# One encoder layer on one core: weight loads moved from SyncE to GpSimd, the splits of the first weights placed behind the first norm, the second half's statistics behind the first features

## Chip, core and metric

The kernel runs on one core of one Trainium2 chip. The metric is the device time of one execution in microseconds. The engines of the core are TensorE (PE in the profile; its weight loads are PEld), VectorE (DVE), ScalarE (ACT), GpSimd (POOL) and SyncE (SP), each with its own instruction queue that is worked off in order. DMA transfers are issued from such a queue (SPq, POOLq) and run on 16 DMA engines.

## What is computed

One layer of a post-norm encoder on 1024 tokens of width 1024, all in float32. Cut to what matters here:

```python
x = layer_norm(x, ln_in_g, ln_in_b)
proj = x @ w_in[l]                       # (1024, 2304): q, k, v of three head groups
qa, ka, va, qb, kb, vb, qc, kc, vc = jnp.split(proj, split_points, axis=-1)
oa = neighbourhood_attention(qa, ka, va, na_rpb[l])        # group A, 4 heads
ob = sliding_window_gqa(qb, kb, vb, sw_sink[l], sw_table)  # group B, 8 query heads, 2 key heads
oc = differential_attention(qc, kc, vc, ...)               # group C, 4 heads
mix = jnp.concatenate([oa, ob, oc], axis=-1) @ w_out[l]
x = layer_norm(alpha * x + mix, ln_mix_g[l], ln_mix_b[l])
hdn = jax.nn.relu(x @ w_ff1[l])
x = layer_norm(alpha * x + (hdn * hdn) @ w_ff2[l], ln_ff_g[l], ln_ff_b[l])
```

## The kernel before

**Precision.** Every float32 operand of a matmul is split in two: a high part (a cast to the format that TensorE takes, `fp32r`) and a low part (the operand less its high part). A product is three matmuls, high x high, high x low and low x high (`mm3`, L144). So every weight block is loaded, cast (`hi`) and subtracted (`lo`) before TensorE can use it.

**The head.** The eight blocks of 128 tokens x0 to x7 are loaded by SP (`load_x`). `ln_half` (L223) takes four of them: statistics on VectorE (L208, L215, L217), a power of -1/2 on GpSimd (L218), the normalisation on ScalarE (L234) or, for two of the first four, on VectorE (L228); then for each of eight column blocks (`dc`) four transposes on TensorE (L239), gain and offset on ScalarE (L241), the high part on VectorE (L246) or ScalarE (L244) and the low part on VectorE (L247). The result `xT[half]` is the feature-major input of all projections. `first_w` (L333) loads the first weights of the queries and keys of group C (QC, KC) and splits them, the cast on VectorE (L338), the subtraction on GpSimd (L339). `split_vc` (L379) splits the value weights of group C: cast on ScalarE (L383), subtraction on VectorE (in the helper `sub`, L130). `t5_vectors` makes position biases, `ln_rows_out` makes the residual rows on GpSimd (L257, L260) and stores them from there (L261).

**The projections.** `feat_pieces` (L344) projects 128 columns of `w_in` in two pieces, one for each half of the tokens; its matmuls are `mm_feat`. `proj_tok` projects values. The first pieces are written out by hand: QC and KC of the first half, then the values of t = 0 to 3, the second half's features, QC and KC of the second half, the values of t = 4 to 7. All other projections (the second blocks of QC and KC, then QA, KA, VA, KB, VB, QB) stand in a list `bg` from which `run_bg` takes pieces at a low priority, as filler work, while the attention runs. Their weights come through `split_w` (L150): SP loads into a tile `raw` that has one buffer, ScalarE casts (L159), GpSimd subtracts (L161; VectorE for the second blocks of QC and KC). `whi` and `wlo` have two buffers each. A load into `raw` can go out only when the subtraction of the weights before has read it; until then SP's queue waits, with all that is behind it. Four blocks of `w_out` (6 and 7 as filler, 4 and 5 in the B stage) go the same way.

**The stages behind.** 32 steps of group C (`c_scores`: scores L471, a fused add and minimum on VectorE L474, exponential on ScalarE L478, the weighted sum of two softmaxes on GpSimd L485, L486 and VectorE L487; three steps later `c_trans` with transposes L500; later `c_values` L515), 16 steps of group A (L618 to L657), 16 of group B (L725 to L763), the output projection, the second norm, and two feed-forward products in seven instead of eight block products (L967 and L1097).

**Order.** The order of the instructions on each queue is made when the kernel is built, by a planner that takes the written order as priority and goes by a model of durations. `tc.issue_after(ins)` adds that instructions traced in its block come behind `ins`, for those on the same engine as `ins` only.

Of the kernel before, what the change touches and what calls it, by code (L numbers as in the profile page):

```python
# [17 lines left out]
P = 128  # L18
# [59 lines left out]
def encoder_kernel(ctx: ExitStack, tc: tile.TileContext, A: dict, out: bass.AP):  # L78
# [71 lines left out]
    def split_w(src_ap, shape, dest=None, raw=None, pool=False):  # L150
        if raw is None:
            raw = sb.tile(shape, F32, tag="raw", bufs=1, name=nm("raw"))
        load(out=raw, in_=src_ap)
        if dest is None:
            hi = sb.tile(shape, F32R, tag="whi", bufs=2, name=nm("whi"))
            lo = sb.tile(shape, F32R, tag="wlo", bufs=2, name=nm("wlo"))
        else:
            hi, lo = dest
        nc.scalar.copy(out=hi, in_=raw)  # L159
        eng = nc.gpsimd if pool else nc.vector  # L160
        eng.tensor_tensor(out=lo, in0=raw, in1=f32(hi), op=ALU.subtract)  # L161
        return hi, lo
# [60 lines left out]
    def ln_half(xs, half, cols):  # L223

        for j in range(4):
            mean, rstd = ln_stats(xs[j])
            if half == 0 and j % 2:
                nc.vector.tensor_scalar(out=xs[j], in0=xs[j], scalar1=mean, scalar2=rstd,  # L228
                                        op0=ALU.subtract, op1=ALU.mult)
# [3 lines left out]
            with (tc.issue_after(last_sub[0].ins) if half else ExitStack()):  # L233
                nc.scalar.activation(out=xs[j], in_=xs[j], func=AF.Identity, scale=rstd, bias=nmr)  # L234
        res = []
        for dc in range(8):
# [11 lines left out]
            if dc < 5:  # L248
                last_sub[0] = lo
            res.append(xp)  # L250
        return res

    def ln_rows_out(xs, rows, ydram):

        with tc.issue_after(last_pow[0].ins):
# [72 lines left out]
    def mm_feat(w, half):  # L328
        pm = ps_mm()
        mm3(pm, [(w[0][:, k, :], w[1][:, k, :], xT[half][k][:, 0, :], xT[half][k][:, 1, :]) for k in range(8)])  # L330
        return pm

    def first_w(base):  # L333
        raw = page([P, 8, P])
        load(out=raw, in_=w_cols(w_in, base, P))
        hi = sb.tile([P, 8, P], F32R, tag="whi", bufs=2, name=nm("whi"))
        lo = sb.tile([P, 8, P], F32R, tag="wlo", bufs=2, name=nm("wlo"))
        nc.vector.tensor_copy(out=hi, in_=raw)  # L338
        nc.gpsimd.tensor_tensor(out=lo, in0=raw, in1=f32(hi), op=ALU.subtract)  # L339
        return hi, lo  # L340

    def feat_pieces(base, f, scale, banded=False, w=None, pool=True):

        w = list(w or ())  # L344
# [57 lines left out]
    def va_pieces():  # L402
        w = []

        def piece(t):
            if not w:
                w.extend(split_v(VA))
# [1049 lines left out]
```

## Time and profile before

| | us |
|---|---|
| median of 3 runs | 1192.36 (1191.1 to 1193.9) |
| profiled execution, whole time | 1192.13 |
| its span, first to last instruction | 1190.4 |
| PE busy in the span | 1141.3 (96%) |
| DVE busy | 953.1 (80%) |
| ACT busy | 642.1 (54%) |
| POOL busy | 414.6 (35%) |
| PE in the chain that ended last | 79% |

Times in the rows are counted from the start of the span. "Busy" is time in which an instruction of the engine ran; matmuls overlap by part of their duration, so the pitch from one start to the next is shorter than the duration of one. A row of the time order has the start, the time until the last of its merged instructions ended, the engine, the line, the operation, output and input tiles with their shapes, the count, and in brackets how long the engine had been idle and what released it.

### The profile page before, as it was taken

How to read it: one execution, taken by the hardware profiler on the slowest of the kernel's cores; microseconds unless marked ns; L12 is line 12 of the kernel's file. 1: busy time of each engine (PE TensorE's matmuls, PEld its weight loads, DVE VectorE, ACT ScalarE, POOL GpSimd, SP SyncE). 2: the span in 40 equal slices, each digit the busy share in tenths (PEclk: the TensorE clock that was granted, in tenths of full speed). 3: DMA queues.
4: the chain of work that ended last, by engine and by line, in shares of the span. 5: the costliest groups of instructions: out<-in, count | busy, mean ns of one | idle time of the engine just before them, and what ended most of it. 6: DMA issues, size and time to landing. Idle time of an engine off the chain costs nothing.

```text
span 1190.4 us, 17144 instructions
## 1 busy us (share of the span) xinstructions
PE 1141.3 (96%) x5642; PEld 947.8 (80%) x5642; DVE 953.1 (80%) x1858; ACT 642.1 (54%) x1253; POOL 414.6 (35%) x368
## 2 busy tenths in 40 slices
PE   3999999999998989998999999999999999999996
PEld 2788889878877878876788888888888888888885
DVE  7566899998656688976779998999774988787985
ACT  4435666666556887765664544445553444444530
POOL 3875666685665775430121222222210000000201
PEclk9999999999989989999999999999999999999998
DMA  8566845362878971214376687766599754355731
GB/s 278 154 237 207 263 143 172 113 171 89 264 212 239 223 168 54 89 71 125 117 237 211 226 277 264 258 246 233 185 333 348 225 197 163 115 164 181 232 122 71
DMA packets 139408, 228.46 MB, mean 192 GB/s; under 512 B 11884, under 2 KB 76300, under 8 KB 139320
## 3 DMA queue, kind: packets, MB, share of 16 engines
q1 hardware_dynamic: 123800, 178.60, 47.7%
q0 software_dynamic: 15520, 48.77, 11.9%
q8 instruction: 45, 0.74, 0.3%
q14 instruction: 43, 0.35, 0.1%
HBM read 157.54 MB, written 77.60 MB: 198 GB/s over the span
## 4 chain that ended last, share of the span: by engine, by line
PE 79%; DVE 5%; ACT 3%; issue 2%; POOL 0%; DMA 0%; SPq 0%; DVEq 0%; ACTq 0%; POOLq 0%
PE psm L144 15%; PE psS L967 11%; PE psS L1097 11%; PE pst L967 7%; PE psm L967 7%; PE pst L1097 5%; PE psm L1097 5%; PE pspv L1097 4%; PE pspv L515 2%; PE psS L471 2%; PE pst L500 2%; PE pspv L754 1%; DVE pg L130 1%; PE pspv L652 1%; PE psS L725 1%
## 5 line engine op out<-in xcount | busy, mean ns | idle before, releaser
L144 PE MATMUL psm<-pg,whi 128*128 128x512 f32 x448 | 153.5, 408 | 2.1 <-DVE pg L246 1.8
L218 POOL TENSOR_TENSOR bnve<-bnve,pw 128x1 f32<-128x1 f32 x24 | 22.5, 940 | 360.7 <-DVE bnve L217 357.5
L1097 PE MATMUL psS<-pg,pg 128*128 128x512 f32 x576 | 140.5, 389 | 0.0
L967 PE MATMUL psS<-pg,pg 128*128 128x512 f32 x576 | 136.2, 393 | 2.4 <-ACT pg L827 2.4
L967 PEld LDWEIGHTS psS<-pg,pg 128*128 128x128 f32 x576 | 108.6, 189 | 25.2 <-ACT pg L827 2.9
L1097 PEld LDWEIGHTS psS<-pg,pg 128*128 128x128 f32 x576 | 108.1, 188 | 22.4
L827 ACT CAST pg<-hr 128x512 fp32r<-128x512 f32 x112 | 69.3, 619 | 95.3 <-PE pst L1097 40.8
L144 PEld LDWEIGHTS psm<-pg,whi 128*128 128x128 f32 x448 | 84.2, 192 | 22.0 <-DVE pg L246 2.2
L478 ACT ACTIVATE pg<-pg,cst 128x1024 f32<-128x1024 f32 x64 | 73.9, 1154 | 51.4 <-DVE cst L474 48.4
L144 PE MATMUL psm<-pg,wlo 128*128 128x512 f32 x224 | 89.7, 401 | 0.8 <-POOL wlo L161 0.8
L967 PE MATMUL psm<-pg,pg 128*128 128x512 f32 x384 | 89.8, 389 | 0.0
L967 PE MATMUL pst<-pg,pg 128*128 128x512 f32 x384 | 89.6, 389 | 0.0
L828 DVE TENSOR_TENSOR pg<-hr,pg 128x512 fp32r<-128x512 f32 x112 | 76.7, 685 | 13.0 <-ACT pg L827 12.9
L967 PEld LDWEIGHTS psm<-pg,pg 128*128 128x128 f32 x384 | 72.1, 188 | 15.0
L967 PEld LDWEIGHTS pst<-pg,pg 128*128 128x128 f32 x384 | 72.1, 188 | 15.0
L130 DVE TENSOR_TENSOR pg<-pst,pg 128x512 fp32r<-128x512 f32 (+2 forms) x112 | 64.9, 589 | 22.6 <-ACT pg L640 8.4
L485 POOL TENSOR_TENSOR pg<-pg,cst 128x704 f32<-128x704 f32 x32 | 49.2, 1537 | 80.1 <-DVE cst L482 52.7
L1097 PE MATMUL pst<-pg,pg 128*128 128x512 f32 x288 | 74.2, 389 | 0.0
L1097 PE MATMUL psm<-pg,pg 128*128 128x512 f32 x288 | 74.2, 389 | 0.0
L975 POOL DMA_DIRECT2D hd<-evb x80 | 43.2, 541 | 86.4 <-DVE evb L823 82.0
L144 PE MATMUL psm<-whi,pg 128*128 128x256 f32 (+1 forms) x256 | 71.5, 346 | 0.8 <-DVE pg L130 0.5
L827 ACT CAST pg<-evb 128x512 fp32r<-128x512 f32 x80 | 48.6, 617 | 39.5 <-DVE evb L823 39.4
(208 smaller groups left out, 2758.8 us busy)
## 6 DMA issues: line engine op xcount, KB each, us to landing
hr<-hd SPq DMA_DIRECT2D x28, 1024.0 KB, 5.7
hd<-evb POOLq DMA_DIRECT2D x80, 256.0 KB, 3.8
w1r<-in_w_ff SPq DMA_DIRECT2D x16, 1024.0 KB
evb<-in_w_ff SPq DMA_DIRECT2D x64, 256.0 KB, 3.7
qk<-evb SPq DMA_DIRECT2D x52, 256.0 KB, 3.9
y<-pg POOLq DMA_DIRECT2D x24, 512.0 KB, 4.4
pg<-y SPq DMA_DIRECT2D x24, 512.0 KB, 5.5
pg<-in_w_ff SPq DMA_DIRECT2D x32, 256.0 KB, 7.8
```

What stands on the lines that cost most here:

```text
L130: nc.vector.tensor_tensor(out=o, in0=a, in1=b, op=ALU.subtract)
L144: mm = nc.tensor.matmul(o, a, b, start=(i == 0), stop=(i == n - 1))
L471: last_mm[0] = nc.tensor.matmul(sc, q[:, m, (i % 2) * P:(i % 2) * P + P], kst[h][kh][:, m, :], start=True, stop=True)
L478: nc.scalar.activation(out=rt, in_=rt, func=AF.Exp, scale=-1.0, bias=sm[:, m:m + 1], accum_out=sm[:, 2 + m:3 + m])
L485: nc.gpsimd.tensor_tensor(out=R[1][:, a], in0=R[1][:, a], in1=sm[:, 6:7].broadcast_to([P, C_POOL]), op=ALU.mult)
L500: nc.tensor.transpose(pt[:, kb * P:(kb + 1) * P], src[:, c0:c0 + P], ident)
L515: nc.tensor.matmul(pv[:, 0:256], Vc[h // 2][kb // 4][:, kb % 4, h % 2, :], src[:, kb % 4, :], start=(n == 0), stop=(n == 15))
L827: nc.scalar.copy(out=pg[:, 0], in_=x)
L828: last_split[0] = nc.vector.tensor_tensor(out=pg[:, 1], in0=x, in1=f32(pg[:, 0]), op=ALU.subtract)
L967: nc.tensor.matmul(o, w[:, e, k], xo[m][k][:, f], start=(n == 0), stop=(n == 11))
L975: nc.gpsimd.dma_start(out=hd_d[m - 1, j], in_=x)
L1097: nc.tensor.matmul(o, h[:, e, sl], w[:, f], start=(k == 0 and n == 0), stop=(k == 15 and n == 2))
```

## The change

Three things. First, `split_w` is replaced by a class `Weights`: a chain in the order of use, in which the load of the next weights is issued right behind the split of those before, from GpSimd's queue where GpSimd did that subtraction, else from SP's. The blocks 6, 7, 4 and 5 of `w_out` are in the chain (`wout_chain`); blocks 0 to 3, which have pages of their own, are loaded by SP as before. Second, `first_w` is taken apart: `first_load` early, `first_split` after `ln_norm` of the first half, with the casts held behind the last normalisation on VectorE (`last_norm`) and the subtractions behind the last power on GpSimd (`last_pow`); the value weights of group C are loaded ahead of x4 to x7 and subtracted on GpSimd, and the first pieces use the low part of their weights last (`lo_last`). Third, `ln_half` is taken apart into `ln_norm` and `ln_feats`, and the second half's statistics are held behind the first half's features up to `dc` = 6 on VectorE.

```diff
-    def split_w(src_ap, shape, dest=None, raw=None, pool=False):
...
+    class Weights:
...
+        def load(self, eng):
+            self.raw = sb.tile(self.shape, F32, tag="raw", bufs=1, name=nm("raw"))
+            eng.dma_start(out=self.raw, in_=self.src)
+
+        def split(self):
+            if self.raw is None:
+                self.load(nc.sync)
+            hi = sb.tile(self.shape, F32R, tag="whi", bufs=2, name=nm("whi"))
+            lo = sb.tile(self.shape, F32R, tag="wlo", bufs=2, name=nm("wlo"))
+            nc.scalar.copy(out=hi, in_=self.raw)
+            eng = nc.gpsimd if self.pool else nc.vector
+            eng.tensor_tensor(out=lo, in0=self.raw, in1=f32(hi), op=ALU.subtract)
+            if self.next:
+                self.next.load(nc.gpsimd if self.pool else nc.sync)
+            return hi, lo
...
-    def ln_half(xs, half, cols):
+    def ln_norm(xs, half):
 
         for j in range(4):
-            mean, rstd = ln_stats(xs[j])
+            with (tc.issue_after(last_sub[0].ins) if half else ExitStack()):
+                mean, rstd = ln_stats(xs[j])
...
-            if dc < 5:
+            if dc < 7:
                 last_sub[0] = lo
...
-        with tc.issue_after(last_pow[0].ins):
+        with tc.issue_after(last_pool[0].ins), tc.issue_after(last_pow[0].ins):
...
+        if lo_last:
+            seq = [(0, e, k) for k in range(8) for e in (0, 1)] + [(1, 0, k) for k in range(8)]
...
+    def first_split(raws):
+
+        ws = []
+        for raw in raws:
+            hi = sb.tile([P, 8, P], F32R, tag="whi", bufs=2, name=nm("whi"))
+            with tc.issue_after(last_norm[0].ins):
+                nc.vector.tensor_copy(out=hi, in_=raw)
+            ws.append((hi, sb.tile([P, 8, P], F32R, tag="wlo", bufs=2, name=nm("wlo"))))
+        for raw, (hi, lo) in zip(raws, ws):
+            with tc.issue_after(last_pow[0].ins):
+                last_pool[0] = nc.gpsimd.tensor_tensor(out=lo, in0=raw, in1=f32(hi), op=ALU.subtract)
+        return ws
...
             nc.scalar.copy(out=hi, in_=raw)
-            sub(lo, raw, f32(hi))
+            with tc.issue_after(last_pool[0].ins):
+                last_pool[0] = nc.gpsimd.tensor_tensor(out=lo, in0=raw, in1=f32(hi), op=ALU.subtract)
...
-    qc = feat_pieces(QC, 0, CSC, w=first_w(QC))
-    kc = feat_pieces(KC, 0, 1.0, w=first_w(KC))
+    first_raws = [first_load(QC), first_load(KC)]
+    raws_vc = load_vc()
     load_x(range(4, NT))
-    raws_vc = load_vc()
     rows_in = ln_rows("ln_in")
-    xT[0] = ln_half(xs[0:4], 0, cols_in)
+    ln_norm(xs[0:4], 0)
+    first_ws = first_split(first_raws)
+    qc = feat_pieces(QC, 0, CSC, w=first_ws[0])
+    kc = feat_pieces(KC, 0, 1.0, w=first_ws[1])
+    xT[0] = ln_feats(xs[0:4], 0, cols_in)
     qc[0]()
     kc[0]()
+    wv = split_vc(raws_vc)
     t5_vectors()
-    wv = split_vc(raws_vc)
...
-    xT[1] = ln_half(xs[4:8], 1, cols_in)
+    ln_norm(xs[4:8], 1)
+    xT[1] = ln_feats(xs[4:8], 1, cols_in)
```

## Rows read from the trace of the kernel before

**Rows 1.** The page: engines' shares in the chain that ended last.

```profile
PE 79%; DVE 5%; ACT 3%; issue 2%; POOL 0%; DMA 0%; SPq 0%; DVEq 0%; ACTq 0%; POOLq 0%
```

**Rows 2.** Busy time by stretch: window, length, PE, PEld, DVE, ACT, POOL, clock, DMA, GB/s.

```profile
11.00:22.00 11.00, 5.05 (x20) 3.85 (x20) 10.22 (x21) 3.86 (x5) 7.57 (x5) 1.00 1.07 384
22.00:30.20 8.20, 6.70 (x19) 5.10 (x20) 7.54 (x18) 6.07 (x8) 3.34 (x4) 1.00 0.56 128
30.20:72.40 42.20, 41.90 (x235) 32.25 (x234) 22.56 (x36) 19.52 (x35) 32.32 (x18) 1.00 0.54 186
150.00:180.00 30.00, 30.00 (x168) 24.70 (x167) 28.17 (x64) 19.67 (x36) 18.93 (x11) 1.00 0.44 144
330.00:390.00 60.00, 52.73 (x300) 44.70 (x299) 36.71 (x97) 36.01 (x87) 37.16 (x31) 0.94 0.81 232
```

**Rows 3.** VectorE in order of time, 11 to 19 us.

```profile
11.05 0.80 DVE L228 TENSOR_SCALAR pg<-pg,bnmv,bnve 128x1024 f32<-128x1024 f32 x1
11.77 0.20 DVE L215 BATCH_NORM_AGGREGATE bnmv<-bnst 128x2 f32<-128x12 f32 x1
...
13.54 2.01 DVE L338 CAST whi<-pg 128x1024 fp32r<-128x1024 f32 x1 [0.71 <-DMA pg<-in_w_in]
...
16.66 2.15 DVE L228 TENSOR_SCALAR pg<-pg,bnmv,bnve 128x1024 f32<-128x1024 f32 x1
```

**Rows 4.** GpSimd in order of time, 11 to 16 us.

```profile
11.21 1.36 POOL L218 TENSOR_TENSOR bnve<-bnve,pw 128x1 f32<-128x1 f32 x1 [0.93 <-DVE bnve L217]
12.61 2.38 POOL L339 TENSOR_TENSOR wlo<-pg,whi 128x1024 fp32r<-128x1024 f32 x1
14.96 0.99 POOL L218 TENSOR_TENSOR bnve<-bnve,pw 128x1 f32<-128x1 f32 x1
```

**Rows 5.** TensorE in order of time, pieces of 22 to 51 us.

```profile
22.04 1.22 PE L144 MATMUL psm<-pg,whi 128*128 128x512 f32 x2 [1.85 <-DVE pg L246]
...
26.45 1.05 PE L144 MATMUL psm<-pg,whi 128*128 128x512 f32 x2
...
30.45 0.40 PE L144 MATMUL psm<-pg,wlo 128*128 128x512 f32 x1
...
50.17 1.15 PE L239 MATMUL psS<-ident,pg 128*128 128x128 f32 x9
```

**Rows 6.** ScalarE, then VectorE, in order of time, 19 to 42 us.

```profile
19.38 0.75 ACT L241 ACTIVATE psS<-psS,ln_in_cols 128x512 f32<-128x512 f32 x1 [5.34 <-PE psS L239]
...
31.02 0.69 DVE L247 TENSOR_TENSOR pg<-psS,pg 128x512 fp32r<-128x512 f32 x1
...
34.96 6.35 DVE L130 TENSOR_TENSOR pg<-pg,pg 128x1024 fp32r<-128x1024 f32 x2
```

**Rows 7.** TensorE's groups from 22 to 30.2 us: busy, mean ns, idle before.

```profile
L144 PE MATMUL psm<-pg,whi 128*128 128x512 f32 x8 | 5.0, 670 | 1.8 <-DVE pg L246 1.8
L144 PE MATMUL psm<-pg,wlo 128*128 128x512 f32 x3 | 1.9, 628 | 0.0
```

**Rows 8.** Loads into tile `raw`: ns of one issue, min/median/max, first and last start.

```profile
L125 SPq DMA_DIRECT2D raw<-in_w_in x14: 373/394/712, 26.6 to 300.6; - x14
L125 SPq DMA_DIRECT2D raw<-in_w_out x4: 333/345/1010, 317.2 to 420.4; - x4
```

**Rows 9.** GpSimd's DMA issues: a group of the page, then order of time.

```profile
L975 POOL DMA_DIRECT2D hd<-evb x80 | 43.2, 541 | 86.4 <-DVE evb L823 82.0
...
52.88 2.31 POOL L261 DMA_DIRECT2D y<-pg  x4
```

**Rows 10.** GpSimd, then TensorE, in order of time around 215 us.

```profile
213.53 1.84 POOL L486 TENSOR_TENSOR pg<-pg,pg 128x704 f32<-128x704 f32 x1
...
216.76 0.60 PE L500 MATMUL pst<-ident,pg 128*128 128x128 f32 x4
```

**Rows 11.** SP's queue, what it waited for: us in total, times, longest.

```profile
SPq L125 <- POOL wlo L161: 35.6, 11, 9.9
```

**Rows 12.** SP's queue in order of time, 350 us.

```profile
350.09 0.34 SPq L125 DMA_DIRECT2D raw<-in_w_out  x1
```

More of the change, by code (lines that the diff above doesn't have):

```diff
@@ L146, in mm3, with __init__ @@
         return mm
-    def split_w(src_ap, shape, dest=None, raw=None, pool=False):
[L151 to L162, printed above, removed]
+    w_chain = []
+    class Weights:
+        def __init__(self, src_ap, shape, pool=True):
+            self.src, self.shape, self.pool, self.raw = src_ap, shape, pool, None
+            self.next = None
+            if w_chain:
+                w_chain[-1].next = self
+            w_chain.append(self)
+        def load(self, eng):
[12 more added lines that the diff above has]
+            return hi, lo
     def w_cols(w, c0, n, k0=0, nk=8):
@@ L232, in ln_half, with ln_feats @@
             nc.vector.scalar_tensor_tensor(out=nmr, in0=mean, scalar=-1.0, in1=rstd, op0=ALU.mult, op1=ALU.mult)
-            with (tc.issue_after(last_sub[0].ins) if half else ExitStack()):
-                nc.scalar.activation(out=xs[j], in_=xs[j], func=AF.Identity, scale=rstd, bias=nmr)
+            nc.scalar.activation(out=xs[j], in_=xs[j], func=AF.Identity, scale=rstd, bias=nmr)
+    def ln_feats(xs, half, cols):
         res = []
@@ L347, in piece @@
             if not w:
-                w.extend(split_w(w_cols(w_in, base + f * P, P), [P, 8, P], pool=pool))
-            pm = mm_feat(w, half)
+                w.extend(ws.split())
+            pm = mm_feat(w, half, first)
             eh = evb([P, 512], F32R)
@@ L368, in feat_pieces @@
         return [lambda: piece(0), lambda: piece(1)]
-    def split_v(c0):
-        return [split_w(w_cols(w_in, c0, 256, 4 * j, 4), [P, 4, 256], pool=True) for j in range(2)]
     def load_vc():
@@ L402, in va_pieces @@
     def va_pieces():
+        ws = [Weights(w_cols(w_in, VA, 256, 4 * j, 4), [P, 4, 256]) for j in range(2)]
         w = []
@@ L406, in piece @@
             if not w:
-                w.extend(split_v(VA))
+                w.extend(x.split() for x in ws)
             e = evb([P, 4, P], F32R)
@@ L418, in piece @@
             if not w:
[L419 removed]
+                w.extend(ws.split())
             pm = mm_feat(w, half)
@@ L771, in encoder_kernel, with wout_chain @@
     last_ab = [None]
+    def wout_chain():
+        for c in (6, 7, 4, 5):
+            w_o[c] = Weights(w_out[c * P:(c + 1) * P, :], [P, D])
     def load_wout(c, paged):
-        dest = None
-        if c < 2:
-            dest = hd_tab()
-        elif paged:
-            dest = page([P, D], F32R), page([P, D], F32R)
-        w_o[c] = split_w(w_out[c * P:(c + 1) * P, :], [P, D], dest, page([P, D]) if paged else None, pool=True)
+        if not paged:
+            w_o[c] = w_o[c].split()
+            return
+        raw = page([P, D])
+        load(out=raw, in_=w_out[c * P:(c + 1) * P, :])
+        hi, lo = w_o[c] = hd_tab() if c < 2 else (page([P, D], F32R), page([P, D], F32R))
+        nc.scalar.copy(out=hi, in_=raw)
+        nc.gpsimd.tensor_tensor(out=lo, in0=raw, in1=f32(hi), op=ALU.subtract)
     def heads_of(t, n):
```

24 lines of the change are left out of this document (14 added, 10 removed).

## Prediction

> **What bounds the kernel now.** I read first the page's chain that ended last, then stretches of the span, then the first 36 us in order of time. The chain is PE for 79% of the span [rows 1]: TensorE is the bound, so a part of this change is worth what it takes out of PE's idle or slow time, or puts there. The stretches say where that lies. Between 150 and 180, in the attention stage, PE is busy 30.00 of 30 us: nothing to win there, only to lose. At the head it is busy 5.05 us of 11 to 22 and 6.70 of 22 to 30.2, then 41.90 of the 42.2 us to 72.4; between 330 and 390 it is busy 52.73 of 60 us [rows 2]. So the place to look is the head up to 30.2 us, and less so 330 to 390.
>
> In the head, time order shows why PE starves. A group of transposes needs x0 to x3 normalised. The statistics of x3 are combined at 11.97 (11.77 + 0.20), but VectorE then runs the two casts of the first weights, the second for 2.01 us from 13.54, and statistics of x4, and normalises x3 only from 16.66 to 18.81, in 2.15 us where the same instruction took 0.80 us for x1 [rows 3]. GpSimd does the same to it: the power for x3 starts at 14.96, when the first weight subtraction (2.38 us from 12.61) is over [rows 4]. PE's first feature matmul starts at 22.04, having waited 1.85 us for a VectorE cast [rows 5], which stood behind statistics of x4 to x7. Up to 30.2 matmuls of 512 columns take 0.63 us [rows 7], from 30.45 on 0.40 us [rows 5]: the durations of the lower and then of the higher of TensorE's two levels (1.2 and 2.4 GHz). The granted clock of these stretches reads 1.00 [rows 2], so for the head the durations are the witness.
>
> **The change part by part.** The profiled execution took 1192.13 us (span 1190.4), the median of the runs is 1192.36; I sum from 1192.1, which stands for both.
>
> *First weights split behind the norm.* Without the casts ahead of it x3 goes on at 11.97: one small VectorE instruction, then the power on GpSimd, free at 12.57 (11.21 + 1.36), for 0.99 us at most [rows 4], so by 13.4; the normalisation then takes 0.80 us, with no subtraction beside it: done at about 14.2 instead of 18.81. The casts follow, one of about 0.80 us, one of 2.01 beside a subtraction [rows 3]; VectorE is free at 17.0. Meanwhile PE does the last ten transposes, ScalarE scales (0.75 us [rows 6]), and VectorE casts the first feature, 17.0 to 17.6. First feature matmul at 17.6 instead of 22.04: **-4.4 us**. Bounds: if the normalisation still meets a subtraction (2.15 us) -3.1, if the second cast misses it -5.6. I take the value between, since the subtraction of the first weights is ready to run as soon as their cast is done.
>
> *Low halves last, statistics of x4 to x7 behind the features.* From 22.04 to 30.2 PE did 19 matmuls [rows 2], 11 of them features [rows 7], 8 transposes. Two in a row took 1.05 us [rows 5], one 0.63, so the pitch is 0.42 us and for a transpose, a quarter of the columns, at most half of that: 11 x 0.42 + 8 x 0.21 = 6.3 us. The other 1.9 of 8.2 us were idle. After the change VectorE has only the features here, 12 casts and subtractions of 0.69 us, 8.3 us, ScalarE 8 x 0.75 us and four casts, at most 8.8 [rows 6]; and while only the high halves of the weights are asked for, each feature feeds four matmuls (1.7 us), so PE stays fed: **-1.9 us**. Bounds: 0 if PE waits for features again, -3.5 if it also reaches the higher level sooner within the same work.
>
> What hides the moved statistics: VectorE gets to them near 25, and with some 1.8 us a row the last of x4 to x7 is normalised near 33. PE asks for them at 50.17 [rows 5], 6 us sooner after the change: a cover of 11 us; gone, each us costs one. x4 to x7 also land behind 1 MB more, 2.7 us at 384 GB/s [rows 2], before they are asked for: nothing.
>
> *Value weights' subtraction to GpSimd.* It takes 6.35 us off VectorE [rows 6] and adds two of 2.38 us [rows 4] on GpSimd; PE was dense throughout [rows 2], so nothing. Behind them on GpSimd wait the residual rows, which are stored and which PE doesn't wait for.
>
> *Weight loads on GpSimd.* Of 18 loads through `raw` (14 + 4 [rows 8]) 15 leave SP for GpSimd; the first three follow weights whose low half VectorE makes, and stay. Each stands behind the subtraction that frees its buffer, so it adds no wait of its own; what queues behind it on GpSimd is the weighted sum of a score step, for which PE's transposes wait. The trace has no GpSimd transfer of 1024 rows of 512 bytes. The nearest rows are stores of 128 rows: 0.54 us for 256 KB, 0.58 each for 512 KB [rows 9]. If the price goes by instruction, 15 x 0.54 = 8.1 us of GpSimd; if by rows, nine loads of 8 x 0.54 = 4.3, two of 2.2 and four of 0.54, 45 us in all. GpSimd is busy 18.93 of 30 us there [rows 2]. The margin of its sums can be small: one is done at 215.37 (213.53 + 1.84), its transposes start at 216.76 [rows 10]. I take nothing, by the rows in which the time doesn't grow with the bytes; bounds -3 (below) and +13 (rival 2).
>
> *SP relieved.* SP's queue stood 35.6 us, in 11 waits, for weight subtractions on GpSimd [rows 11]. PE's dense stages show no place where it waits for that, so I take zero. The Trainium skill, "DMA: Bandwidth & Descriptors", section "Issuing engines are not separate DMA queues", says that issuing from several engines saves only the time to issue; that would be 15 x 0.39 us of a queue that is not the bound, also zero, while the row shows that waiting in order is the larger part of it.
>
> Sum: 1192.1 - 4.4 - 1.9 = **1185.8 us**, if PE stays dense from its new start on, as it is from 30.2 to 72.4 now.
>
> **The rivals.**
> *1. The relief of SP pays too.* At 350.09 SP issues a load of `w_out` that had waited for a subtraction, with loads of values behind it [rows 12], in the stretch in which PE is idle 7.3 of 60 us at a granted clock of 0.94 [rows 2]. One such wait (35.6 / 11 = 3.2 us) and the time lost at the lower level (0.06 x 60 = 3.6 us) would give 1185.8 - 6.8 = 1179.0. Against: fewer waits on SP don't make GpSimd and VectorE faster, and they work in that stretch too.
> *2. GpSimd becomes the bound: slower.* Place: the score steps. A weight load comes about every 20 us (14 in 26.6 to 300.6 [rows 8]), so the idle 11.1 of 30 us are used up when a load takes more than 11.1 / 1.5 = 7.4 us; but by 1.4 us it can already reach PE where the margin is that of [rows 10]. At 4.3 us nine loads cost at most 9 x 2.9 = 26 us, half of it if half of the steps have margins above 4.3: +13, 1199. For: neighbours stretch each other here (0.80 against 2.15 us [rows 3]). Against: PE has filler work, and [rows 9]. The Trainium skill, "SBUF — State Buffer", section "SBUF: two separate sides", speaks against the move too: GpSimd can't write its DMA descriptors while VectorE runs a two-port copy, 3.1 us instead of 0.62; as an estimate by that page 15 loads would hold GpSimd 47 us, the dear end again. No row here has a GpSimd load beside such a copy.
> *3. The gain is given back.* The order behind is made in advance, and what arrives 6 us early may meet its data late between 330 and 390, where PE isn't dense: 1190 to 1194.7. That the head's order comes out as before belongs here: 1192.
>
> **How the numbers follow.** Forecast 0.54 (1181 to 1189.9, the bounds of the head); rival 1 0.13; rival 3 0.18; rival 2 0.09; the gain lost and a further stretch at the lower level met, 3.6 us as priced above, 0.06. About 0.2% (2.4 us) is what a measurement here can tell from no change. So faster 0.67, same 0.18, slower 0.15. The range leaves out the dear end of rival 2 and the best of rival 1: 1177 to 1196.
>
> **What would show it.** Right: x3 normalised by 14.5, first feature matmul near 17.6, matmuls of 0.40 us before 25, later stages shifted by the same 6 us. Wrong: GpSimd loads above 2 us with transposes waiting for sums; PE idle between 25 and 60; a head that is 6 us shorter and an end that is not.

## The result and the profile after

| | before | after |
|---|---|---|
| median, us | 1192.35 (1191.1 to 1193.9) | 1208.76 (1206.47 to 1208.92) |
| ratio, 95% interval | | 1.0136 [1.0118, 1.0153] |
| span of the profiled execution | 1190.4 | 1204.7 |
| first product of `c_scores` | 87.0 | 92.9 |
| last product of `c_scores` | 309.4 | 324.3 |

The change makes the kernel slower by 16.4 us; the forecast was 1185.8, faster by 6.3. The traces were taken of one execution each, and the one of after (1206.47 us) was its quickest, so they show 14.3 us of the difference. The stretches of after, with the columns of [rows 2] (window, length, PE, PEld, DVE, ACT, POOL, clock, DMA, GB/s):

```profile
11.00:22.00 11.00, 8.80 (x44) 6.49 (x44) 9.00 (x16) 7.83 (x12) 5.62 (x3) 1.00 1.06 386
22.00:30.20 8.20, 8.20 (x36) 4.65 (x35) 6.41 (x20) 5.33 (x8) 5.99 (x5) 1.00 0.51 121
30.20:72.40 42.20, 28.61 (x181) 23.95 (x179) 30.96 (x25) 15.68 (x27) 42.16 (x24) 0.91 0.58 185
72.40:90.00 17.60, 14.79 (x85) 13.25 (x86) 8.01 (x15) 4.44 (x9) 4.04 (x5) 0.83 0.81 269
...
210.00:300.00 90.00, 83.72 (x501) 72.11 (x501) 82.19 (x188) 55.59 (x105) 60.08 (x39) 0.96 0.43 119
330.00:390.00 60.00, 54.56 (x305) 45.76 (x303) 37.11 (x96) 33.30 (x82) 40.60 (x34) 0.94 0.77 239
```

The head is what the change was to make of it: PE is busy 8.80 and 8.20 us where [rows 2] has 5.05 and 6.70. Then, from 30.2 to 72.4, it is busy 28.61 us where it had been busy 41.90. For the score stage, the stretch from 210 to 300 of before, to be read against the one of after:

```profile
210.00:300.00 90.00, 88.02 (x526) 74.75 (x525) 84.75 (x197) 57.89 (x108) 61.01 (x38) 1.00 0.45 130
```

The head of after in order of time, VectorE and then TensorE (start, us, engine, line, operation):

```profile
11.91 0.81 DVE L244 TENSOR_SCALAR pg<-pg,bnmv,bnve 128x1024 f32<-128x1024 f32 x1 [0.66 <-POOL bnve L233]
12.64 1.29 DVE L369 CAST whi<-pg 128x1024 fp32r<-128x1024 f32 x2
...
15.50 0.72 PE L353 MATMUL psm<-pg,whi 128*128 128x512 f32 x2 [1.13 <-DVE pg L264]
```

x3 is normalised at 12.72 instead of 18.81, in 0.81 us, and the first feature matmul starts at 15.50 instead of 22.04 [rows 3, 5]. Where the time went shows in order of time from 53 to 76 us, all engines (lines between left out):

```profile
53.41 1.78 POOL L281 DMA_DIRECT2D y<-pg  x3
...
54.71 0.69 DVE L265 TENSOR_TENSOR pg<-psS,pg 128x512 fp32r<-128x512 f32 x1
...
55.21 9.35 POOL L280 TENSOR_TENSOR pg<-pg,pg 128x1024 f32<-128x1024 f32 x4
55.31 19.12 DVE L331 TENSOR_TENSOR lq<-lq,lk 128x64 f32<-128x64 f32 x1
...
58.51 1.09 PE L353 MATMUL psm<-pg,whi 128*128 128x512 f32 x4
64.51 0.58 POOL L281 DMA_DIRECT2D y<-pg  x1
65.11 9.22 POOL L280 TENSOR_TENSOR pg<-pg,pg 128x1024 f32<-128x1024 f32 x4
...
74.48 0.68 DVE L265 TENSOR_TENSOR pg<-pst,pg 128x512 fp32r<-128x512 f32 x1
...
75.21 0.80 PE L353 MATMUL psm<-pg,whi 128*128 128x512 f32 x1 [15.62 <-DVE pg L265]
```

A product of 64 columns on VectorE (L331, parameters of group C) lasts 19.12 us. It ends at 74.43, when GpSimd's eighth residual instruction does (65.11 + 9.22 = 74.33). Behind it in VectorE's queue stands the last subtraction of the second half's features, at 74.48, for which PE waits 15.62 us. The eight instructions of L280 on x4 to x7 are called the second row below, those on x0 to x3 the first. In before the same product met nothing. GpSimd, then VectorE, of before, in order of time (the rows that answer to these):

```profile
65.07 20.89 POOL L260 TENSOR_TENSOR pg<-pg,pg 128x1024 f32<-128x1024 f32 x8 [9.88 <-PE pst L239]
...
63.59 0.22 DVE L311 TENSOR_TENSOR lq<-lq,lk 128x64 f32<-128x64 f32 x1
...
72.90 2.74 DVE L161 TENSOR_TENSOR wlo<-raw,whi 128x1024 fp32r<-128x1024 f32 x1 [4.60 <-ACT whi L159]
```

GpSimd had to pause for 9.88 us until PE had transposed the last of x4 to x7 (the second row overwrites them); the product took 0.22 us in that pause, and what VectorE ran later beside the row lasted 2.83 us at most. After the change the transposes are done 11 us earlier, GpSimd goes from its stores into the second row with no pause, and VectorE is shut out for the whole of it.

The sum of the loss: `c_scores`, the score steps of group C, could have begun 9.8 us earlier (it does in e9, below, where only the stall is missing), and begins 5.9 later: 15.7 us, the stall. Some 1.2 us of that come behind it: the granted clock fell while PE stood idle (0.91 and 0.83 in the rows above), and then the first eight products with a low half took 3.26 us, at the lower level, the next eight 2.02. The score stage then takes 324.3 - 92.9 = 231.4 us where before took 222.4: another 9.0. What follows gives back 0.6, which makes the span's 14.3.

For what PE waits within the score stage (us in total, times, longest; before, then after):

```profile
PE psS L471 <- DVE cst L474: 1.2, 3, 0.6
```

```profile
PE psS L509 <- DVE cst L512: 5.2, 6, 1.9
```

These are the score products themselves, waiting for VectorE's fused add and minimum of an earlier step. With smaller waits PE waits 7.3 us there in after and 2.5 in before, 4.8 of the 9.0. The granted clock reads 0.91 from 230 to 250 and 0.92 from 270 to 290, where before has 1.00; priced as in the prediction, by the missing share, that is an estimated 3.4 us more at most.

The weight loads, by line (ns of one, min/median/max, first and last start), and what SP's queue waited for (us in total, times, longest):

```profile
L165 POOL DMA_DIRECT2D raw<-in_w_in x11: 777/911/960, 108.2 to 312.0; - x11
L165 POOL DMA_DIRECT2D raw<-in_w_out x4: 585/610/2431, 338.6 to 442.0; - x4
```

```profile
SPq L125 <- POOL wlo L174: 6.1, 1, 6.1
```

SP's waits for subtractions fall from 35.6 us [rows 11] to 6.1, and a load costs GpSimd 0.6 to 0.9 us in the middle.

### The profile page after: what moved, and what is told of

Same layout as the page of the kernel before. It is cut to its first block, busy times and chain, and to the rows that moved or that the text cites. A ratio compares the mean times of both kernels' runs of the same rounds, so it can differ in the third digit from the quotient of the medians.

```text
span 1204.7 us, 17131 instructions
## 1 busy us (share of the span) xinstructions
PE 1143.8 (95%) x5642; PEld 948.6 (79%) x5642; DVE 964.9 (80%) x1856; ACT 642.8 (53%) x1253; POOL 425.7 (35%) x385
## 4 chain that ended last, share of the span: by engine, by line
PE 81%; DVE 8%; ACT 4%; issue 3%; DMA 2%; POOL 1%; SPq 0%; DVEq 0%; ACTq 0%; POOLq 0%
PE psm L144 16%; PE psS L1141 11%; PE psS L1011 11%; PE pst L1011 7%; PE psm L1011 7%; PE psm L1141 5%; PE pst L1141 5%; PE pspv L1141 4%; PE pspv L553 2%; PE pst L144 2%; PE psS L509 2%; PE pst L538 2%; DVE lq L331 2%; PE psm L353 1%; DVE pg L130 1%
## 5 line engine op out<-in xcount | busy, mean ns | idle before, releaser
L144 PE MATMUL psm<-pg,whi 128*128 128x512 f32 x384 | 128.9, 406 | 0.0
L872 DVE TENSOR_TENSOR pg<-hr,pg 128x512 fp32r<-128x512 f32 x112 | 77.2, 689 | 14.9 <-ACT pg L871 14.7
L144 PEld LDWEIGHTS psm<-pg,whi 128*128 128x128 f32 x384 | 72.4, 192 | 15.2
L144 PE MATMUL psm<-pg,wlo 128*128 128x512 f32 x192 | 77.0, 402 | 0.0
```

The costliest lines, as they stand in the source:

```text
L144: mm = nc.tensor.matmul(o, a, b, start=(i == 0), stop=(i == n - 1))
L872: last_split[0] = nc.vector.tensor_tensor(out=pg[:, 1], in0=x, in1=f32(pg[:, 0]), op=ALU.subtract)
```

## The experiments

Each is after with one or two edits, unless it says before. "Held" is a VectorE instruction that lasts over 12 us beside a row of GpSimd. In the expectations A is that this hold, set up by the shorter head, costs the time. Times of one kernel spread more here than before's do, so ranges are given; e2 shows one reason.

**Whose instruction is held.** e1 gives the product to GpSimd, e2 also puts all weight loads back on SP.

```diff
-        nc.vector.tensor_tensor(out=lq, in0=lq, in1=lk, op=ALU.mult)
+        nc.gpsimd.tensor_tensor(out=lq, in0=lq, in1=lk, op=ALU.mult)
```

> The changed kernel with one instruction on another engine: the product lq = lq*lk (128x64, both operands in SBUF) is made by GpSimd instead of VectorE. In the changed kernel that product holds VectorE for 19.12 us from 55.31, until GpSimd's row of eight residual products and sums is over (74.33), and PE stands from 59.6 to 75.21. Theory A, VectorE can't read its two SBUF operands while GpSimd works through that row without a pause: off VectorE the product costs nothing, PE is busy over 40 of the 42.2 us from 30.2 to 72.4, the feature groups follow each other, and the time falls by 12 to 20 us, to 1189 to 1197. Rival B, the product waited for something of its own (its two operands' transfers): then GpSimd waits in its place, its residual rows start later and the time stays above 1203. Rival C, the later loss of some 9 us between 180 and 290 comes from the idle stretch at 60 to 75: then it is gone too and the time is 1180 to 1186; if it comes from the weight loads on GpSimd or the new order, it stays.

```diff
-                self.next.load(nc.gpsimd if self.pool else nc.sync)
+                self.next.load(nc.sync)
```

> As the run before it, and the 15 weight loads that the change put on GpSimd are issued by SP again, at the same place behind the split of the weights in use. Theory D, loads on GpSimd cost nothing but their 0.91 us of GpSimd each, which its idle time covers: within 2 us of the run before. Rival E, the load stands between the subtraction and the next weighted sum (0.30 us of waiting and 0.91 us, 15 times, 18 us of GpSimd at most, of which a third or more reaches PE): 4 to 10 us faster than the run before. Rival F, SP's queue is what was relieved: slower than the run before by 2 us or more, with waits on SP for GpSimd's subtractions.

e1: 1206.78 us (1194.36 to 1210.96), ratio 1.0104 [1.0030, 1.0177]. e2: 1206.06 (1193.88 to 1209.42; three of nine runs near 1194, six above 1202), 1.0084 [1.0047, 1.0121]. GpSimd, then VectorE, of e1:

```profile
53.88 1.78 POOL L281 DMA_DIRECT2D y<-pg  x3
...
55.68 19.13 DVE L340 TENSOR_SCALAR negsink<-sink 128x8 f32<-128x8 f32 x1
```

The hold goes to the next small instruction, a scaling of 8 columns with one input, which none of the three theories had said. So it is not the product, nor its two operands. The profiled execution of e2 was one of the three quick ones (1194.84):

```profile
59.18 9.49 POOL L280 TENSOR_TENSOR pg<-pg,pg 128x1024 f32<-128x1024 f32 x4 [3.29 <-PE pst L257]
68.61 0.58 POOL L281 DMA_DIRECT2D y<-pg  x1
...
60.63 0.97 DVE L340 TENSOR_SCALAR negsink<-sink 128x8 f32<-128x8 f32 x1
...
75.28 2.54 DVE L174 TENSOR_TENSOR wlo<-raw,whi 128x1024 fp32r<-128x1024 f32 x1 [3.52 <-ACT whi L172]
```

Here GpSimd paused 3.29 us ahead of the row, and nothing was held: 0.97 us, and 2.54 even behind the store inside the row. The pause was there because PE was late: it had been busy without a gap, 8.20 of 8.20 us from 22 to 30.2, yet from 30 to 36 its granted clock was 0.50, the lower of its two levels, and the second half's transposes began at 45.25 where they begin at 40.30 in e1.

```profile
30.00:36.00 6.00, 6.00 (x13) 2.34 (x13) 3.03 (x5) 4.09 (x4) 6.00 (x7) 0.50 0.02 7
```

So 5 us lost on TensorE in the head gave GpSimd its pause back and saved the stall. The other quick executions have no trace; that they are quick for the same reason is not shown.

**Which part of the change.** e3 is before with the chain of weights alone, loads on GpSimd; e4 is after without the loads behind the splits, so all of them go on SP.

```diff
-    def split_w(src_ap, shape, dest=None, raw=None, pool=False):
+    class Weights:
...
+            if self.next:
+                self.next.load(nc.gpsimd if self.pool else nc.sync)
```

> The kernel before with only the chain of weights of the change: each weight is loaded behind the split of the one in use, 15 of the loads issued by GpSimd; the head (first splits, statistics, value weights, features) is that of before. Theory D: 1190 to 1194, no difference. Rival E, GpSimd's loads reach PE: 1196 to 1202, with lost PE time between 180 and 300. The product lq = lq*lk stays on VectorE at 63.6 where GpSimd pauses (55.2 to 65.07), so it takes about 0.2 us under every theory.

```diff
-            if self.next:
-                self.next.load(nc.gpsimd if self.pool else nc.sync)
```

> The changed kernel with the weights loaded as before (each load issued by SP at the place of its split); the head is that of the change, the product lq = lq*lk on VectorE. Theory A: the long product is a matter of the head alone, so it takes over 15 us here too, and the time is over 1200. If the chain of weights had a part in it, the product is short and the time 1184 to 1190.

e3: 1198.85 us (1197.1 to 1200.62), 1.0052 [1.0034, 1.0070]; no hold; its score stage lasts 85.5 to 318.7, 233.2 us. e4: 1208.7 (1197.52 to 1209.01), 1.0112 [1.0064, 1.0160]; the product held for 19.11 us. The stall belongs to the head, and not to the loads; with the old head the chain with its loads on GpSimd costs 6 us of its own.

**When VectorE arrives.** e5 repeats one subtraction of the second half's features, which brings the product 0.7 us later:

```diff
-            lo = nc.vector.tensor_tensor(out=xp[:, 1, :], in0=pt, in1=f32(xp[:, 0, :]), op=ALU.subtract)
+            for _ in range(1 + (half and dc == 4)): lo = nc.vector.tensor_tensor(out=xp[:, 1, :], in0=pt, in1=f32(xp[:, 0, :]), op=ALU.subtract)
```

> The changed kernel with one subtraction more on VectorE: the low half of the fifth feature of the second half is computed twice (same result), 0.60 us of VectorE ahead of the product lq = lq*lk. In the changed kernel that product starts 0.10 us behind the first of GpSimd's eight row instructions and lasts until the last; in a second kernel (the product on GpSimd) the stall moved to the next small VectorE instruction, that started with the row (19.13 us for 128x8). Theory A1, only a VectorE instruction that meets the very start of the row is held to its end, one that comes in the middle of an instruction waits for the end of that one: the product now starts some 0.6 us after the row's start, takes 2.4 us at most, and the kernel is FASTER by 10 us or more although work was added: 1190 to 1199. Rival A2, any two-operand product of VectorE in SBUF is held as long as GpSimd's row lasts: still over 15 us long, time above 1203. Where PE works at its lower level in the first 40 us, everything comes some 5 us later and the start is not met anyhow.

1198.23 us (1195.09 to 1199.2), 1.0044 [1.0024, 1.0065]. VectorE of e5, for a row that began at 55.33:

```profile
56.00 18.55 DVE L331 TENSOR_TENSOR lq<-lq,lk 128x64 f32<-128x64 f32 x1
```

Still held, 0.67 us into the row's first instruction: meeting it at its start isn't what decides. The time fell into the range of theory A1, but not by its mechanism: the hold is there, and `c_scores` begins at 93.8, no earlier than in after. What is better lies behind, where the planner made another order: PE is busy 89.32 of 90 us from 210 to 300, where after has 83.72.

**All the small ones away.** e6 takes six small instructions off VectorE, e7 adds loads on SP, e8 keeps six loads on GpSimd.

```diff
-        nc.vector.tensor_tensor(out=lq, in0=lq, in1=lk, op=ALU.mult)
-        nc.vector.tensor_reduce(out=lam[:, 0:2], in_=lq, op=ALU.add, axis=AX.X)
+        nc.gpsimd.tensor_tensor(out=lq, in0=lq, in1=lk, op=ALU.mult)
+        for j in range(2):
+            nc.scalar.activation(out=lk[:, j, :], in_=lq[:, j, :], func=AF.Identity, accum_out=lam[:, j:j + 1])
...
-        nc.vector.tensor_scalar(out=negsink, in0=sink, scalar1=-1.0, scalar2=None, op0=ALU.mult)
+        nc.gpsimd.tensor_scalar(out=negsink, in0=sink, scalar1=-1.0, scalar2=None, op0=ALU.mult)
```

> The changed kernel with all six small instructions on lq, lk, g and sink off VectorE (product, difference and the three scalings on GpSimd ahead of its rows, the sum over 32 elements on ScalarE with its accumulator). Theory A: no VectorE instruction between 45 and 75 reads SBUF alone, so none is held: no idle stretch of PE of over 3 us between 30 and 90 in any run, the first score step starts near 75, and the time is the same in all runs, 1189 to 1195: the head's 10 to 12 us less some 7 us that the weight loads on GpSimd cost between 210 and 300 (PE busy 83 to 84 of these 90 us instead of 88). Rival G, the stall has another cause in the head (clock, features): two levels of time stay.

> As the run before it, with the 15 weight loads issued by SP at the same places. Theory A with E: the 7 us between 210 and 300 come back (PE busy 88 of 90 us), but between 90 and 150 a weight load waits in SP's queue behind tables and keys, ScalarE waits for it with exponentials behind (PE busy 55 to 56 of 60 us), 5 us: about the same time as the run before it, 1186 to 1192. Rival D, the loads' queue doesn't matter: same order of waits, within 1 us of the run before it.

```diff
-                self.next.load(nc.gpsimd if self.pool else nc.sync)
+                self.next.load(nc.gpsimd if self.pool and w_chain.index(self) < 8 else nc.sync)
```

> As e6, but only the first 6 of the 15 loads (up to about 200 us) are issued by GpSimd, the other 9 by SP. If the gain of GpSimd's loads lies ahead of 150 us and their cost behind 210 us, this takes both: 1180 to 1186, faster than every kernel so far and than the kernel before by 6 us or more. If the cost is a matter of the planned order alone, it may show anywhere: 1186 to 1195.

e6 1206.23 us (1204.02 to 1207.81), 1.0116 [1.0088, 1.0144]; e7 1205.91 (1204.75 to 1207.63), 1.0116 [1.0089, 1.0143]; e8 1202.66 (1202.1 to 1205.48), 1.0092 [1.0065, 1.0120]. All three missed what was expected, 1195 us at most: they are held at VectorE's next instruction that reads no PSUM, a weight's low half; in e6:

```profile
62.73 14.78 DVE L174 TENSOR_TENSOR wlo<-raw,whi 128x1024 fp32r<-128x1024 f32 x1 [5.44 <-PE psm L353]
```

Instructions that read PSUM (tiles `psm`, `psS`, `pst`) are not held: beside the first row of after, 34.64 to 53.49, VectorE ran nothing else, at 0.68 or 0.69 us for 512 columns as without a row. So in these kernels whatever VectorE first asks of SBUF alone beside the second row waits for the row's end, and removing it only passes the hold on.

**The row itself.** e9 leaves every instruction but puts the eight stores behind both rows, on GpSimd alone; e10 is e9 with e4's edit.

```diff
+            for k, op in enumerate((ALU.mult, ALU.add)): last = nc.gpsimd.tensor_tensor(out=xs[t], in0=xs[t], in1=rows[k], op=op)
+        with tc.issue_after(last.ins):
+            for t in range(NT): nc.gpsimd.dma_start(out=ydram[t], in_=xs[t])
```

> The changed kernel with GpSimd's eight stores of the residual rows behind the last of its 16 row instructions; four of them stood in front of and inside the second row. Nothing else moves: the instructions of all other engines and their order are those of the changed kernel. In all traces so far VectorE was held over 4 us (14 to 19 us in six kernels) only where GpSimd went from a DMA of its own into its row without a pause; where the row followed a pause of 3 us or more (the kernel before, the second kernel of these experiments) or had no DMA before it, VectorE got in at the end of the GpSimd instruction it met. Theory H, the DMA ahead of the row makes the difference: the product lq takes 2.5 us at most, PE is busy over 40 of the 42.2 us from 30.2 to 72.4, and the time falls by 14 us or more, to 1188 to 1195 (the loss of some 7 us between 210 and 300 stays, since the order there is the same). Rival A2, the length of the row makes it: the product is held for the whole second row, over 15 us, and the time stays above 1203.

> The head of the change alone (weights loaded by SP at their splits, as in e4) with the eight stores behind the rows; all other engines keep the order of e4, which took 1208.7. Against e9 it tells what the 15 loads on GpSimd are worth without the stall. Theory H: no VectorE instruction held over 3 us before 90: 14 us or more less than e4, 1189 to 1195. If the loads on GpSimd cost 6 us as with the head of before (e3: 1198.9 against 1192.7), this is 3 to 8 us faster than e9's 1191.2, 1183 to 1188; if ScalarE's wait for a late weight in the 90 to 150 stretch (PE busy 55.8 of 60 us in e4) costs as much, the two are equal within 2 us.

e9: 1191.22 us (1182.93 to 1198.49), 0.9981 [0.9956, 1.0006]. e10: 1190.58 (1188.88 to 1193.48), 0.9980 [0.9967, 0.9993]. GpSimd, VectorE, and one stretch of e9:

```profile
54.68 20.88 POOL L279 TENSOR_TENSOR pg<-pg,pg 128x1024 f32<-128x1024 f32 x8 [0.53 <-PE pst L257]
...
55.96 1.21 DVE L331 TENSOR_TENSOR lq<-lq,lk 128x64 f32<-128x64 f32 x1
...
57.16 2.32 DVE L340 TENSOR_SCALAR negsink<-sink 128x8 f32<-128x8 f32 x1
...
30.20:72.40 42.20, 41.41 (x261) 35.27 (x261) 26.07 (x39) 20.45 (x35) 41.67 (x21) 1.00 0.56 186
```

No hold: the instructions wait for the end of the one GpSimd instruction that they meet, and PE is busy 41.41 of 42.2 us. With the order of all other queues unchanged (the traces have the same instructions in the same order there), the stores' place alone takes 17.5 us off. It also leaves GpSimd a pause of 0.53 us ahead of the second row, since no stores fill that time; e16, below, has an open second row without one. Why single executions of e9 differ by 15 us is open. But the head's gain doesn't reach the end. `c_scores` begins at 77.2, 9.8 us ahead of before, and ends at 308.7, 0.7 ahead. e10 comes to the same time within about 3 us (the two intervals), so with this head no worth of the loads on GpSimd shows either way.

**The same hold in the kernel before.** e11 moves one store of before, that of row 3, behind the first instruction of the second row; e14 puts a scaling of one column there instead.

```diff
+            o = nc.gpsimd.tensor_tensor(out=xs[t], in0=xs[t], in1=rows[0], op=ALU.mult)
+            with (tc.issue_after(o.ins) if t == 4 else ExitStack()): t == 4 and nc.gpsimd.dma_start(out=ydram[3], in_=xs[3])
```

> The kernel before with one GpSimd instruction moved by one place: the store of the fourth residual row stands behind the first instruction of the second row (L260 at 65.07) instead of ahead of it, where GpSimd then pauses for 9.88 us. All other engines keep their order. Theory H: the row now goes on directly behind a DMA, and VectorE's small product on lam near 67, or the low half of a weight at 72.76, is held until the row's end near 86 instead of 2.7 us: PE runs dry, and the kernel is SLOWER than before by 5 to 19 us: 1198 to 1212. Rival A2 or any theory by which the head of the change is needed for the stall: the DMA costs GpSimd its 0.58 us and nothing else, 1190 to 1194.

```diff
+            with (tc.issue_after(o.ins) if t == 4 else ExitStack()): t == 4 and nc.gpsimd.tensor_scalar(out=warm, in0=warm, scalar1=1.0, scalar2=None, op0=ALU.mult)
```

> The kernel before with one GpSimd instruction more, a scaling of a 128x1 tile (0.25 us), behind the first instruction of the second row; the stores stand where they stood, all other engines keep their order. In e11 a store at this place made the low half of a weight hold VectorE for 12.57 us; in e12 a small instruction was held 18.59 us by a row that had a 128x1 scaling of GpSimd (0.24 us) and no DMA ahead of it. Theory H, only a DMA of GpSimd closes the row: 1190 to 1195, no instruction of VectorE held over 3.5 us before 90. Theory I, any instruction of another kind (or a short one) in the chain of GpSimd's work closes it: one held for 10 us or more between 66 and 90, and the time 1203 to 1211.

e11: 1207.62 us (1207.07 to 1210.37), 1.0131 [1.0104, 1.0157]. e14: 1193.07 (1191.08 to 1197.31), 1.0008 [0.9994, 1.0022]. GpSimd, VectorE and TensorE of e11, then VectorE of e14:

```profile
66.44 0.59 POOL L260 DMA_DIRECT2D y<-pg  x1
...
71.90 12.57 DVE L161 TENSOR_TENSOR wlo<-raw,whi 128x1024 fp32r<-128x1024 f32 x1 [4.60 <-ACT whi L159]
...
85.13 1.22 PE L144 MATMUL psm<-pg,whi 128*128 128x512 f32 x2 [8.62 <-DVE evb L363]
```

```profile
70.84 2.96 DVE L161 TENSOR_TENSOR wlo<-raw,whi 128x1024 fp32r<-128x1024 f32 x1 [4.60 <-ACT whi L159]
```

This is the cleanest run of the study: with nothing of the change in it, one store moved by one place costs 15 us and makes the same instruction last 12.57 us instead of 2.74. In before, e11 and e14 that instruction starts 7.83 us behind the row's start, so its arrival is the same in all three. A small instruction in the store's place does nothing.

**The first row.** e12 is e8, and e15 is after with e8's six loads, both with the stores last; e13 is e5 with the stores last; e16 is e12 with the scaling of `lam` (128 x 1, on GpSimd there) moved behind the rows.

> The kernel of e8 (small instructions on lq, lk, g and sink off VectorE, first 6 weight loads issued by GpSimd, the other 9 by SP) with the eight stores behind the rows; all other engines keep the order of e8. There the low half of a weight (L174 at 61.99) held VectorE for 14.80 us. Theory H: it takes 2.8 us at most, and the 1202.7 us fall by 10 to 15 to 1187 to 1193. Rival A2: above 1200.

> The kernel of e5 (one subtraction computed twice; all 15 weight loads by GpSimd) with the eight stores behind the rows; all other engines keep the order of e5, whose planned order lost nothing between 210 and 300 (PE busy 89.32 of 90 us, with the same loads on GpSimd) and in which lq held VectorE for 18.55 us. Theory H: no instruction of VectorE is held over 3 us before 90, and the 1198.2 us fall by 14 to 19, to 1179 to 1184: faster than the kernel before by 0.7 to 1.1%. Rival A2: above 1195.

> The changed kernel with two edits: the eight stores behind the rows (e9) and only the first 6 of the 15 weight loads issued by GpSimd, the other 9 by SP. The score products ran from 77.2 to 308.7 in e9 (231.5 us, all 15 loads on GpSimd) and from 78.2 to 304.7 in e10 (226.5, none); in the two kernels with six loads they took 220.1 and 221.0 (e8 from 92.8, e12 from 93.8). If the early loads are worth having on GpSimd and the late ones not: start at 77 to 78, 220 to 224 us of scores, and 1191.2 - 8 to 11 = 1180 to 1184. If these differences are a matter of the planned order alone: 1183 to 1192, as e9 and e10.

```diff
+        with tc.issue_after(last_row[0].ins):
+            nc.gpsimd.tensor_scalar(out=lam[:, 3:4], in0=lam[:, 2:3], scalar1=-LAM_INIT, scalar2=None, op0=ALU.add)
```

> The kernel of e12 with one GpSimd instruction moved: the 128x1 scaling of lam, that stood right ahead of the first row (35.82, 0.24 us), stands behind the second. All other engines keep their order. In e12 a small instruction of VectorE that started at 36.01, while that scaling ran, was held for 18.59 us, with no DMA ahead of the row. If the scaling closed that row: the instruction takes 2.4 us at most and the time falls from 1206.2 by 12 to 19, to 1187 to 1194. If not (e14's scaling inside the second row of the kernel before closed nothing), the hold stays and the time is above 1202.

| | us | ratio, 95% interval | `c_scores` | lasts |
|---|---|---|---|---|
| e9 | 1191.22 | 0.9981 [0.9956, 1.0006] | 77.2 to 308.7 | 231.5 |
| e12 | 1206.16 (1204.15 to 1206.53) | 1.0107 [1.0086, 1.0128] | 93.8 to 314.8 | 221.0 |
| e13 | 1182.03 (1179.58 to 1186.6) | 0.9914 [0.9885, 0.9943] | 78.3 to 302.7 | 224.4 |
| e15 | 1192.31 (1187.51 to 1198.07) | 1.0005 [0.9988, 1.0022] | 77.2 to 307.1 | 229.9 |
| e16 | 1187.92 (1187.22 to 1189.24) | 0.9964 [0.9949, 0.9978] | 77.4 to 297.3 | 219.9 |

e12 was expected to be free of the hold and wasn't. GpSimd and VectorE of e12, then VectorE of e16 at the same place:

```profile
35.82 0.24 POOL L336 TENSOR_SCALAR lam<-lam 128x1 f32<-128x1 f32 x1
36.01 18.59 DVE L248 SCALAR_TENSOR_TENSOR nmr<-bnmv,bnve 128x1 f32<-128x1 f32 x1 [0.15 <-ACT evb L400]
...
36.03 18.55 POOL L279 TENSOR_TENSOR pg<-pg,pg 128x1024 f32<-128x1024 f32 x8
```

```profile
34.78 1.36 DVE L248 SCALAR_TENSOR_TENSOR nmr<-bnmv,bnve 128x1 f32<-128x1 f32 x1 [0.50 <-ACT evb L402]
```

In e12 the first row holds VectorE, with no store ahead of it; the second row, which followed a pause, didn't. So a row can be shut with no store ahead of it. Moving the GpSimd instruction of 0.24 us from there takes 18.2 us off (e16), with all other queues in the same order, and the four times of each kernel lie far apart. That the scaling shut the row is still not shown: in e16 the small VectorE instruction came earlier, at 34.78, met the instruction ahead of the row and not the row, and in e8, with the scaling in its place, one that came at 34.34 lasted 1.38 us. It came late in e12 because TensorE did (granted clock 0.79 from 28 to 36; 1.00 in e8 and e16). e13 is the fastest kernel of the study, faster than before and after: no hold, and 89.24 of 90 us busy from 210 to 300:

```profile
210.00:300.00 90.00, 89.24 (x508) 75.33 (x507) 75.03 (x185) 57.09 (x103) 63.93 (x41) 1.00 0.55 153
```

Its one superfluous subtraction is no reason in itself: it makes the planner lay out the score stage in another order, which lasts 7.1 us less than that of e9. e15 says that this is not the late loads on GpSimd: without them the stage still takes 229.9 us. What differs is the wait shown for before and after above: score products wait 4.6 to 5.2 us for VectorE in after, e9 and e15, the stages of 230 to 232 us, and 0.5 us or nothing in e13 and e16.

## Why the prediction was wrong, point by point

**The step that failed** is the sum's last clause, "if PE stays dense from its new start on", and the sentence on which it leaned: "Behind them on GpSimd wait the residual rows, which are stored and which PE doesn't wait for." PE does wait for them, through VectorE. The terms of the sum were right in sign and place; the stall of 15.6 us isn't in any of them, and no rival is it. The 9.0 us that the score stage takes longer break the same clause: the text had later stages "shifted by the same 6 us". Under "what would show it wrong" the text had "PE idle between 25 and 60; a head that is 6 us shorter and an end that is not". The second came; the idle time came right behind the window named, from 59.6 to 75.21.

**What could have been read before.** The profile showed GpSimd's pause of 9.88 us, that it ended with PE's transposes, and that VectorE's small instructions ran in it. It also showed neighbours that stretch each other, 0.80 against 2.15 us [rows 3], which I used in the head alone. Six us taken from the head are six us taken from that pause. That they would meet could be foreseen; the price could not: the longest VectorE instructions beside a row in before lasted 3.0 and 3.4 us (the two of [rows 6]), and the 19.12 us of after have no row there. The Trainium skill, "SBUF — State Buffer", section "SBUF: two separate sides", says that VectorE and GpSimd share a pair of ports, and that whichever takes it keeps it for the whole instruction. The instructions of 1.2 to 3.4 us in e9, e14 and before agree with that; the holds of 12.6 to 19.1 us, over up to eight instructions and through a store's issue (64.51 in after), last longer than it says.

**The first weights' split behind the norm.** Forecast -4.4 with bounds of -3.1 and -5.6; the first feature matmul came 6.5 us earlier. The mis-sized term is the two casts: the text gave the second 2.01 us beside a subtraction, and both took 1.29 together, since no subtraction ran beside them. (By its own rows the power for x3 ends by 13.56 and not 13.4, a slip of 0.2 us.) Some 1.3 us of the gain may be no effect at all: in e3, e11 and e14, with the head of before, the first transposes come 1.2 us earlier than in before's profiled execution, and the first feature matmul at 20.7 to 20.8. The 9.8 us of e9 have such a part too: in e14 `c_scores` begins at 85.2.

**Low halves last, statistics behind features.** The 1.9 us were right in kind: PE is busy 8.20 of 8.20 us from 22 to 30.2, with 36 matmuls for 19. The second half's transposes start at 40.1 instead of 50.17 [rows 5], 10 us earlier where the two terms give 6.3. The cover of the moved statistics was there: x4 to x7 are normalised by 36.0 (34.73 + 1.24 on ScalarE), said to be near 33. The two terms' bounds add up to 1183.0 to 1189.0; the 1181 to 1189.9 that the text calls the bounds of the head are wider.

**Value weights' subtraction on GpSimd.** Priced at nothing, and I find no cost of its own; it was not undone alone, so this is not shown.

**Loads on GpSimd.** Priced at nothing between -3 and +13. With the head of before they and their chain cost 6 us (e3), with the new head and no hold nothing that shows (e9 against e10). One issue took 0.9 us of GpSimd for the weights of `w_in`, near the 0.54 us per instruction and far from 4.3. The same section of the Trainium skill gives 3.1 us for a transfer issued by GpSimd beside a VectorE copy; of 15 issues one came near, 2.43 us. How much of the 6 us is the issues and how much another planned order isn't settled: the score stage takes 224 to 233 us with all loads on GpSimd, 222 to 228 with none, 220 to 230 with six, and orders differ in each. Rival 2 had a time of that kind (1199), but the loss of after is at another place.

**SP relieved.** Zero, and it was: 29.5 us of waits vanish and no time follows in e9 against e10. In e10 one cast waited 6.03 us for a late weight, so SP's order isn't free everywhere:

```profile
121.11 1.05 ACT L172 CAST whi<-raw 128x1024 fp32r<-128x1024 f32 x1 [6.03 <-DMA raw<-in_w_in]
```

**Rival 3**, the gain given back, had 0.18 and holds for the rest: with the hold away (e9), a lead of 9.8 us at the start of the scores is 0.7 at their end. It was placed between 330 and 390; the loss is in the score stage. e13 and e16 keep 6.7 and 12.1 us of lead to that end, so it is the order laid out for that stage. In the slow ones PE waits for VectorE's step of the scores; why the planner's order makes it late there stays open.

**What stays open** of the hold is its rule. Shown are single moves: a store moved into the row shuts it (e11), stores moved behind it open it (e9, e10 against e4, e13 against e5), and a tiny instruction inside a row does nothing (e14). Whether one directly ahead of a row shuts it (e12, e16) is not shown. Against a simple rule on stores stands e2, where a store inside the row, behind four of its instructions, left it open. The second rows that GpSimd entered right behind stores were shut (after, e1, e4 to e8); those entered after a pause of 0.5 us or more were open, except that of e11, where the store came after the pause; that of e16, entered from the first row with neither pause nor store between, was open.

## What to carry over

Before work is moved forward, list the idle pauses of every engine behind it that the move will close, and what runs on other engines within them: the pause of an engine that PE "doesn't wait for" can be what lets another engine through. A long row of SBUF-to-SBUF instructions on GpSimd can shut VectorE's SBUF-only instructions out for its whole length, so keep the last VectorE step ahead of TensorE clear of it, or try the stores behind the row. Where the order is laid out by a planner, an edit of no cost can move the time by 7 us, so a part's price needs runs in which only that part moves.

## What the runs showed of the hardware

Unexpected: a VectorE instruction of 8 columns lasted 19.13 us beside eight GpSimd instructions of 2.4 us each (e1), where the same row with no store ahead let it through after 2.32 us (e9). In the held form the eight instructions run unstretched (9.35 and 9.22 us for four), in the open form they take 20.88 us for eight: GpSimd loses some 2 us when it lets VectorE in, and VectorE loses up to 19 when it doesn't. Beside rows of either form VectorE's instructions that read 512 columns of PSUM took 0.68 or 0.69 us.

Also unexpected: TensorE's granted clock fell to its lower level (0.50 from 30 to 36 in e2) right behind a stretch in which it had no gap, and there the slower engine made the kernel faster.
